# 192 unread TensorE products behind the last product of a two-layer decoder trunk

## The chip, the cores and the metric

The kernel runs on one core of a Trainium2 chip. The metric is the device time of one execution in microseconds (us), lower is better. Five engines work side by side on their own instruction streams: TensorE (PE in the profile; its weight loads are listed apart as PEld), VectorE (DVE), ScalarE (ACT), GpSimd (POOL) and SyncE (SP), which issues most of the DMA transfers.

## The reference

The reference is a decoder trunk of two layers on 256 positions of width 2048, all in float32. The first layer is a Mamba-2 mixer, the second a sliding-window attention with sinks; each ends in a LayerNorm of `ALPHA * x + mixer(x)`. The change concerns nothing that is computed; what stands next to it is the end of the second layer:

```python
def _layernorm(x, g, b):
    mu = jnp.mean(xf, axis=-1, keepdims=True)
    var = jnp.mean(jnp.square(xf - mu), axis=-1, keepdims=True)
    y = (xf - mu) * lax.rsqrt(var + EPS) * g.astype(jnp.float32) + b.astype(jnp.float32)
...
    o = _swa_sink_attention(q, k, v, sinks.reshape(KV_HEADS, Q_PER_KV))
    o = o * jax.nn.silu(gate)
    return o @ w_out
...
        x = _layernorm(ALPHA * x + h, ln_g[layer], ln_b[layer])
```

## The kernel before

**Split products.** Weights come from DRAM in units of 128 x 2048 float32. Each unit is split into two float32r tiles: `wh`, the rounded value (ScalarE, line 178), and `wl`, the rest (VectorE, line 181). Activations are split in the same way (`xH`/`xL`, `x1H`/`x1L`, `yH`/`yL`, `oH`/`oL`). A product of two float32 matrices is then three float32r products, high by high, high by low and low by high, added up in a PSUM tile. Every product loads its own stationary operand.

**Two forms.** In the projections (`narrow` and `mac`, line 265) the weights are stationary, 128 columns of them, and 256 columns of activations move. In the output products (`out_unit`, line 339) the activations are stationary and 512 columns of weights move; the last output tile is done in two halves of 256 columns.

**Places.** The tiles `wh` and `wl` are 2112 elements (8448 bytes) wide: 2048 of a unit and 64 to spare. In most units the data begin at byte 0 of the tile (`WHOLE`). In the attention projections they begin at 64 bytes modulo 256 for all but the first blocks (`BROKEN`, `BROKEN2`). The activation tiles `xH` and `xL` are laid by `Split` so that all but the first block begin at 192 modulo 256; the other activation tiles named above begin at 0.

**The order.** The tile framework schedules what is not pinned by `keep_in_program_order` (`ordered` in the last part); the last part is pinned throughout. `out_last` (line 353) goes over four output tiles `nb` for the first 128 positions and then for the second, with `behind` after each: it takes LayerNorm statistics and, behind the last tile of a half, the norm and the stores. For the second half that is `last` (line 1436): three `ax` PSUM tiles get `b` of the norm by a product with the identity (line 1444), then `t` times the diagonal matrix `dg` (line 1453), while VectorE does the other column blocks (lines 1416 and 1423). The results are stored by SyncE and ScalarE (line 1411). The pool `ax` has four buffers. After the program's own instructions SyncE waits for every DMA queue's count and for the count of each other engine, and a barrier of all engines closes the program (line 1580).

Of the kernel before, what the change touches and what calls it, by code (L numbers as in the profile page):

```python
# [9 lines left out]
F32R = mybir.dt.float32r  # L10
BF16 = mybir.dt.bfloat16
# [6 lines left out]
P = 128  # L18
# [79 lines left out]
def trunk(ctx: ExitStack, tc: tile.TileContext, A: dict, out: bass.AP, dbg=None):  # L98
    nc = tc.nc
# [20 lines left out]
    def mm_tile():  # L120
        return mm_ps.tile([P, 512], F32, tag="mm", name=nm("mm"), bufs=4)
# [136 lines left out]
    def next_unit(behind=False):  # L258
        load_next(min(used[0] + 1 + AHEAD, len(srcs)) - len(units), behind, not behind)
        used[0] += 1  # L260
        return units[used[0] - 1]
# [60 lines left out]
    def pinned(m, pin):  # L322
        if pin:
            tc.keep_in_program_order(m)

    def out_unit(aH, aL, h, u, nb, first, rms=None, pin=False, c0=0, c1=512, add=None, low_last=False):

        ps = mm_tile()[:, : c1 - c0]
        hs = slice(h * P, (h + 1) * P)
        if add is not None:  # L330

            for i in range(2):
                pinned(nc.tensor.matmul(ps, add[0], add[1 + i], start=i == 0, stop=False), pin)
        steps = [(k, a, l) for k in range(4) for a, l in ((aH, 0), (aL, 0), (aH, 1))]
        if low_last:
            steps.sort(key=lambda s: s[1] is aL)
        for n, (k, a, l) in enumerate(steps):
            ks = slice(k * 512 + c0, k * 512 + c1)
            pinned(nc.tensor.matmul(  # L339
                ps, a[:, k, hs], (u.h, u.l)[l][:, ks], start=n == 0 and add is None, stop=n == 11  # L340
            ), pin)
        v = xr[:, h, nb * 512 + c0 : nb * 512 + c1]
        if add is not None:
            return ps
        if first:
            nc.vector.scalar_tensor_tensor(v, v, ALPHA, ps, ALU.mult, ALU.add)
        elif rms is not None:
            nc.vector.scalar_tensor_tensor(v, ps, rms[:, h : h + 1], v, ALU.mult, ALU.add)
        else:
            pinned(nc.vector.tensor_tensor(v, v, ps, ALU.add), pin)  # L350

    def out_last(aH, aL, behind, add):


        us = []
        for nb in range(4):
            us.append(next_unit())
            out_unit(aH, aL, 0, us[nb], nb, False, low_last=nb == 0)
            behind(0, nb)
        for nb in range(4):  # L360

            n = 256 if nb == 3 else 512
            for c0 in range(0, 512, n):
                ps = out_unit(aH, aL, 1, us[nb], nb, False, None, True, c0, c0 + n, add if nb == 3 and c0 else None)
                behind(1, nb, c0, c0 + n, ps)
# [638 lines left out]
    us = {}  # L1004
# [80 lines left out]
    for h in range(2):  # L1085
        ps = mm_tile()
# [317 lines left out]
    ordered = tc.keep_in_program_order  # L1404
# [57 lines left out]
    def behind(h, nb, c0=0, c1=512, v=None):  # L1462
        ordered(norm_stats(st2, h, nb, c0, c1, v))
        if (h, nb) == (0, 3):
            sc[0] = norm_scale(bp, st2, 0, 4)
            centre(0, 0)
            nmr = bp.tile([P, 1], F32, tag="nmr", name="nmr")
            ordered(nc.vector.tensor_scalar(nmr[:], sc[0][0][:, 0:1], sc[0][1][:], -1.0, ALU.mult, ALU.mult))
            scale(0, 0)
            for c in range(1, 4):  # L1470
                norm_aside(0, c, nmr)
        elif (h, nb) == (1, 1):
            norm_aside(0, 3, None)
        elif (h, c0 + c1) == (1, 768):
            last(v)
# [7 lines left out]
    nc.scalar.activation(rH, v, AF.Copy)  # L1483
    nc.vector.tensor_tensor(rL, v, rH.bitcast(F32), ALU.subtract)
    out_last(*os_[3], behind, (one, rH, rL))


def _layout(inputs):
    import numpy as np
# [94 lines left out]
```

## Time and profile before

| | us |
|---|---|
| time, median of 2 runs (975.04 to 975.18) | 975.11 |
| span of the profiled execution, first to last instruction | 973.8 |
| outside the span (median less span) | 1.3 |
| TensorE busy | 965.5 |
| VectorE busy | 786.6 |
| ScalarE busy | 671.4 |

The page of the profile names the span of its execution; the two timed runs are executions of the same program, and the time that each takes in all is that of the table's first row. The time of a matrix product in the profile runs from its start to its modelled end; since products are pipelined, neighbours overlap, and the step from start to start is what one costs. A row of the chain of waits names its start, how long it lasted, the engine, what was written, the line and how many instructions; a timeline row names start, length, engine, line, operation, output and inputs. The granted TensorE clock was 1.000 in the mean of the span.

### The profile page before, as it was taken

How to read it: one execution, taken by the hardware profiler on the slowest of the kernel's cores; microseconds unless marked ns; L12 is line 12 of the kernel's file. 1: busy time of each engine (PE TensorE's matmuls, PEld its weight loads, DVE VectorE, ACT ScalarE, POOL GpSimd, SP SyncE). 2: the span in 40 equal slices, each digit the busy share in tenths (PEclk: the TensorE clock that was granted, in tenths of full speed). 3: DMA queues.
4: the chain of work that ended last, by engine and by line, in shares of the span. 5: the costliest groups of instructions: out<-in, count | busy, mean ns of one | idle time of the engine just before them, and what ended most of it. 6: DMA issues, size and time to landing. Idle time of an engine off the chain costs nothing.

```text
span 973.8 us, 18857 instructions
## 1 busy us (share of the span) xinstructions
PE 965.5 (99%) x7332; PEld 892.0 (92%) x7332; DVE 786.6 (81%) x1217; ACT 671.4 (69%) x1282; POOL 119.1 (12%) x202
## 2 busy tenths in 40 slices
PE   9999999999999999999999999999999999999998
PEld 8999989998999999999899899888999988898976
DVE  7978898896977877787797687889977769778778
ACT  7675884884785686487477579467777776884772
POOL 0000403102110310310300121411000000000002
PEclk9999999999999999999999999999999999999999
DMA  9689467676656666576476654568654545456542
GB/s 359 237 290 337 147 216 228 212 230 203 218 192 220 205 205 206 167 237 213 152 250 203 216 178 155 187 190 265 193 174 158 185 138 186 153 177 213 205 143 86
DMA packets 61273, 197.90 MB, mean 203 GB/s; under 512 B 6800, under 2 KB 11328, under 8 KB 60928
## 3 DMA queue, kind: packets, MB, share of 16 engines
q1 hardware_dynamic: 58528, 188.53, 59.1%
q0 software_dynamic: 2048, 7.65, 2.4%
q8 instruction: 57, 0.93, 0.4%
q10 hardware_dynamic: 608, 0.52, 0.2%
q14 instruction: 32, 0.26, 0.1%
HBM read 194.45 MB, written 2.23 MB: 202 GB/s over the span
## 4 chain that ended last, share of the span: by engine, by line
PE 75%; DVE 10%; ACT 6%; DMA 5%; issue 3%; SPq 1%; DVEq 0%; ACTq 0%
PE mm L265 48%; PE mm L339 20%; DVE wl L181 4%; DMA wr<-in_wa 2%; PE mm L1052 2%; PE ax L670 2%; ACT wh L178 2%; DMA wr<-in_wb 1%; ACT p L1248 1%; DMA xr<-in_first 1%; DVE cv L510 1%; ACT e L566 1%; ACT ptw L1281 1%; ACT pt L1281 0%; DMA rscr<-f 0%
## 5 line engine op out<-in xcount | busy, mean ns | idle before, releaser
L181 DVE TENSOR_TENSOR wl<-wr,wh 128x1024 fp32r<-128x1024 f32 (+2 forms) x354 | 391.5, 1126 | 87.8 <-ACT wh L178 86.0
L178 ACT ACTIVATE wh<-wr 128x1024 fp32r<-128x1024 f32 (+2 forms) x354 | 332.9, 974 | 95.9 <-PE mm L265 50.9
L265 PE MATMUL mm<-xH,wh 128*128 128x256 f32 x1280 | 354.6, 277 | 0.1
L265 PE MATMUL mm<-xH,wl 128*128 128x256 f32 x1280 | 353.8, 276 | 0.0
L265 PE MATMUL mm<-xL,wh 128*128 128x256 f32 x1280 | 353.7, 276 | 0.0
L265 PEld LDWEIGHTS mm<-xH,wh 128*128 128x128 f32 x1280 | 240.3, 188 | 2.3 <-issue 1.0
L265 PEld LDWEIGHTS mm<-xL,wh 128*128 128x128 f32 x1280 | 240.4, 188 | 1.0
L265 PEld LDWEIGHTS mm<-xH,wl 128*128 128x128 f32 x1280 | 240.3, 188 | 0.1
L265 PE MATMUL mm<-x1H,wh 128*128 128x256 f32 x512 | 142.2, 278 | 2.1 <-DVE sg L1186 2.1
L265 PE MATMUL mm<-x1L,wh 128*128 128x256 f32 x512 | 141.6, 277 | 0.0
L265 PE MATMUL mm<-x1H,wl 128*128 128x256 f32 x512 | 141.5, 276 | 0.0
L339 PE MATMUL mm<-wh,yH 128*128 128x512 f32 x256 | 100.8, 394 | 0.1
L339 PE MATMUL mm<-wh,yL 128*128 128x512 f32 x256 | 99.8, 390 | 0.0
L339 PE MATMUL mm<-wl,yH 128*128 128x512 f32 x256 | 99.7, 390 | 0.0
L265 PEld LDWEIGHTS mm<-x1H,wh 128*128 128x128 f32 x512 | 96.1, 188 | 3.6 <-DVE sg L1186 2.4
L265 PEld LDWEIGHTS mm<-x1L,wh 128*128 128x128 f32 x512 | 96.2, 188 | 0.1
L265 PEld LDWEIGHTS mm<-x1H,wl 128*128 128x128 f32 x512 | 96.2, 188 | 0.0
L510 DVE SCALAR_TENSOR_TENSOR cv<-mm,pc,cv 128x255 f32<-128x255 f32 x144 | 68.4, 476 | 4.6 <-ACT cv L508 2.5
L686 POOL TENSOR_TENSOR yz<-yz,z 128x256 f32<-128x256 f32 x32 | 26.7, 843 | 259.2 <-DVE yz L681 259.2
L339 PEld LDWEIGHTS mm<-wl,yH 128*128 128x128 f32 x256 | 48.1, 188 | 10.3
L339 PEld LDWEIGHTS mm<-wh,yH 128*128 128x128 f32 x256 | 48.1, 188 | 9.7 <-issue 0.3
L339 PEld LDWEIGHTS mm<-wh,yL 128*128 128x128 f32 x256 | 48.1, 188 | 9.0
(247 smaller groups left out, 1262.8 us busy)
## 6 DMA issues: line engine op xcount, KB each, us to landing
wr<-in_wa SPq DMA_DIRECT2D x154, 512.0 KB, 5.2
wr<-in_wo SPq DMA_DIRECT2D x64, 512.0 KB, 4.4
wr<-in_wq SPq DMA_DIRECT2D x32, 512.0 KB, 4.4
wr<-in_wg SPq DMA_DIRECT2D x31, 512.0 KB, 4.8
wr<-in_wb SPq DMA_DIRECT2D x16, 512.0 KB, 4.0
wr<-in_wb SPq DMA_DIRECT2D x32, 256.0 KB, 4.3
rb<-rscr SPq DMA_DIRECT2D x11, 512.0 KB, 5.4
wr<-in_wkv SPq DMA_DIRECT2D x8, 512.0 KB, 5.7
```

The costliest lines, as they stand in the source:

```text
L178: m = nc.scalar.activation(h[:, sl], v, AF.Copy)
L181: m = nc.vector.tensor_tensor(l[:, sl], v, h[:, sl].bitcast(F32), ALU.subtract)
L265: m = nc.tensor.matmul(ps, a, b, start=first and i == 0, stop=last and i == 2)
L339: pinned(nc.tensor.matmul(ps, a[:, k, hs], (u.h, u.l)[l][:, ks], start=n == 0 and add is None, stop=n == 11), pin)
L510: nc.vector.scalar_tensor_tensor(a[:, sft:], ps[:, : S - sft], w(3 - sft), a[:, sft:], ALU.mult, ALU.add)
L566: m = nc.scalar.activation(e[:, h, cols], rb[:, h, c * P :], AF.Relu, scale=-1.0, bias=rtk[:, c, h0 + h : h0 + h + 1])
L670: nc.tensor.matmul(ps[64 * r : 64 * r + 64, cols], st.xd[:, c, i, 64 * r : 64 * r + 64], e[:, 256:] if c else e[:, :256], start=c == 0, st ...
L686: nc.gpsimd.tensor_tensor(v, v, st.z[i][:], ALU.mult)
L1052: m = nc.tensor.matmul(ps[:], (x1H, x1L, x1H)[i][:, kk, hs], (u.h, u.h, u.l)[i][:, ks], start=(kk, i) == (0, 0), stop=ui == 3 and (k, i) = ...
L1248: nc.scalar.activation(byhead[:, r], byhead[:, r], AF.Exp, bias=ng[:, r : r + 1], accum_out=rs[:, r : r + 1])
L1281: nc.scalar.copy(to[32 * c : 32 * c + 32].rearrange("p r a -> p (r a)"), src[32 * i : 32 * i + 32, cc_].rearrange("p r b -> p (r b)"),)
```

## The change

Behind the last part of the kernel 192 products are written. They read the split weights of the third unit of `out_last`, `wh` as moving and `wl` as stationary operand, each from its 64th element on (256 bytes), and all write one more `ax` tile, each as a complete product (`start` and `stop` set). Nobody reads it. `at` is the offset of the moving operand in bytes, `w_at` that of the stationary one. Eleven values of `at` and six other pairs are taken with 512 columns, six products each, eight of the same values of `at` with 256 columns, eight products each. Then come six products with 64 and six with 32 stationary columns, and six and eight with both operands read as bfloat16, 512 and 256 columns. `last_units` only makes the units of `out_last` known outside it.

```diff
+    last_units = []
+
     def out_last(aH, aL, behind, add):
-        us = []
+        us = last_units
         for nb in range(4):
             us.append(next_unit())
...
     out_last(*os_[3], behind, (one, rH, rL))
+
+    mv, st = last_units[2].h, last_units[2].l
+    ps = ax_tile()
+
+    def unread(times, n, at, w_at, m=P, dt=F32R):
+        per = 4 if dt is F32R else 2
+        for _ in range(times):
+            a, b = mv[:, 64:1088].bitcast(dt), st[:, 64:320].bitcast(dt)
+            ordered(nc.tensor.matmul(
+                ps[:m, :n], b[:, w_at // per : w_at // per + m], a[:, at // per : at // per + n], start=True, stop=True
+            ))
+
+    for at in (0, 16, 32, 48, 64, 96, 128, 160, 192, 224, 240):
+        unread(6, 512, at, 0)
+    for at, w_at in ((0, 32), (0, 64), (0, 128), (0, 192), (64, 64), (64, 128)):
+        unread(6, 512, at, w_at)
+    for at in (0, 32, 64, 96, 128, 160, 192, 224):
+        unread(8, 256, at, 0)
+    unread(6, 512, 0, 0, 64)
+    unread(6, 512, 0, 0, 32)
+    unread(6, 512, 0, 0, P, BF16)
+    unread(8, 256, 0, 0, P, BF16)
```

The end of TensorE's stream before; `t` and `gb` are the tiles of the last norm, `cc` holds the identity:

```order
L339 MATMUL mm_11412<-wl_11273,oH_11166 128x256
L1444 MATMUL ax_11428<-gb_1_11236,cc 128x256
L1444 MATMUL ax_11429<-gb_1_11236,cc 128x256
L1444 MATMUL ax_11430<-gb_1_11236,cc 128x512
L1453 MATMUL ax_11428<-t_11442,dg 128x256
L1453 MATMUL ax_11429<-t_11442,dg 128x256
L1453 MATMUL ax_11430<-t_11450,dg 128x512
L1580 UNCONDITIONAL_BRANCH
```

The last product of a norm block is followed by the branch to the closing barrier. The same place in the changed kernel, where these lines stand two further down and `x102` counts equal rows in a run; the bfloat16 products at the end have weight loads of their own, of which the first pair is shown:

```order
L339 MATMUL mm_11412<-wl_11273,oH_11166 128x256
L1446 MATMUL ax_11428<-gb_1_11236,cc 128x256
L1446 MATMUL ax_11429<-gb_1_11236,cc 128x256
L1446 MATMUL ax_11430<-gb_1_11236,cc 128x512
L1455 MATMUL ax_11428<-t_11442,dg 128x256
L1455 MATMUL ax_11429<-t_11442,dg 128x256
L1455 MATMUL ax_11430<-t_11450,dg 128x512
L1496 MATMUL ax_11465<-wh_11245,wl_11246 128x512 x102
L1496 MATMUL ax_11465<-wh_11245,wl_11246 128x256 x64
L1496 MATMUL ax_11465<-wh_11245,wl_11246 64x512 x6
L1496 MATMUL ax_11465<-wh_11245,wl_11246 32x512 x6
L1496 LDWEIGHTS wl_11246
L1496 MATMUL ax_11465<-wh_11245,wl_11246 128x512
```

The new products stand behind the last product of the norm, line 1453 before and 1455 now, and ahead of the branch to the closing barrier. Nothing else changes place on any engine.

## The prediction

> **What bounds the kernel now.** I read the page first, then the chain of waits, then the last ten microseconds in the timeline, because the change stands there.
>
> ```profile
> span 973.8 us, 18857 instructions
> PE 965.5 (99%) x7332; PEld 892.0 (92%) x7332; DVE 786.6 (81%) x1217; ACT 671.4 (69%) x1282; POOL 119.1 (12%) x202
> PE 75%; DVE 10%; ACT 6%; DMA 5%; issue 3%; SPq 1%; DVEq 0%; ACTq 0%
> L265 PE MATMUL mm<-xH,wh 128*128 128x256 f32 x1280 | 354.6, 277 | 0.1
> L339 PE MATMUL mm<-wh,yH 128*128 128x512 f32 x256 | 100.8, 394 | 0.1
> ```
>
> TensorE bounds nearly all of it: 99% busy, 75% of the chain, and its big groups wait for nothing (0.1 us). What a product costs is not the 277 or 394 ns of its own time, since the next one begins before it ends. It is the distance from start to start, which the chain of waits gives for long unbroken stretches:
>
> ```profile
> 321.86 27.23 PE mm L265 x240
> 349.09 5.45 PE mm L339 x24
> 354.54 10.91 PE mm L265 x96
> ...
> 835.64 32.99 PE mm L265 x288
> ```
>
> 27.23 / 240 = 0.1135 us for a product of 256 columns, 5.45 / 24 = 0.227 us for one of 512. These are split float32 (float32r) products, and each loads its own stationary operand; the loads are hidden. Now the end:
>
> ```profile
> 964.07 0.28 PE L339 MATMUL mm<-wh,oL 128*128 128x256 f32 x1
> ...
> 965.27 0.28 PE L339 MATMUL mm<-wl,oH 128*128 128x256 f32 x1
> 965.39 1.88 PE L1444 MATMUL ax<-gb,cc 128*128 128x256 f32 x6
> 967.39 1.99 PE L1453 MATMUL ax<-t,dg 128*128 128x256 f32 x6
> 969.42 0.58 ACT L1454 COPY xr<-ax 128x512 f32<-128x512 f32 x1 [0.49 <-PE ax L1453]
> 970.01 0.88 DVE L1423 SCALAR_TENSOR_TENSOR xr<-t,rs,gb 128x256 f32<-128x256 f32 x2
> L1411 SPq DMA_DIRECT2D out<-xr x8: 332/333/400, 958.9 to 970.9; - x8
> DMA to landing us min/median/max: 1.9/2.0/2.1
> SPq L1580 <- DMA out<-xr: 1.1, 3, 0.4
> ```
>
> TensorE ends at 967.39 + 1.99 = 969.38. VectorE ends at 970.89, the last store is issued at 970.9 and lands 2.0 later, at 972.9; SyncE waits for it (last row), and the closing barrier of all engines takes the 0.9 to 973.8. So TensorE stands idle for the last 4.4 us, and that is all the cover that work put behind its last product can have. The median of the two runs is 975.11, so 1.3 us lie outside the span of the profiled execution; I carry them over unchanged.
>
> **The change part by part.** Nothing is removed or moved. One engine, TensorE, gets 192 products behind the L1453 ones. The moving operand is `wh`, the stationary one `wl`, of the third unit of the last output block; both were written and used before 963, so nothing is waited for. The target is an `ax` buffer that the end of the kernel does not hold. Nobody reads the results; but SyncE's closing waits include TensorE's count, which now comes with the last of the 192. No instruction of another engine changes place, so the stores are as before and are over by 972.9.
>
> *How many.* With 512 columns: 11 x 6 at eleven places of the moving operand, 6 x 6 at other places of the stationary one, 6 each with 64 and 32 stationary columns, 6 bfloat16: 66 + 36 + 12 + 6 = 120. With 256 columns: 8 x 8 and 8 bfloat16: 72.
>
> *Where they start.* A product begins about 0.16 before its predecessor's time ends (0.28 long and 0.12 apart in the 964 rows). So the first begins near 969.38 - 0.16 = 969.22. TensorE is the engine that finishes earliest here; from 969.22 on every product moves its end, and from about the 16th (972.9) the end of the kernel.
>
> *What one costs.* The rows show that the place matters. Both `wh` and `wl` are 8448 bytes wide, 33 x 256, and start at multiples of 256 bytes in the built program, so offsets can be told modulo 256. The first stretches with 256 columns have the moving `xH`, `xL` at 192 and the stationary weights at 0: 0.1135. The stretch from 835.64 has the moving `x1H`, `x1L` at 0 and nearly all weights at 64: 32.99 / 288 = 0.1145. The 964 rows have both operands at 0: (965.27 - 964.07) / 10 = 0.120. The 512-column rows of L339 have both at 0 as well: 0.227. The floor is what streaming alone takes. The six L1444 passes are full float32, at half rate: 4 of 256 and 2 of 512 columns, 2048 columns in 1.88 - 0.16 = 1.72 us, 0.84 ns a column, so 0.42 at full rate, 0.215 for 512 and 0.1075 for 256. A float32r product thus pays 0.006 over the floor at a good pair of places and 0.012 with both at 0. I take that excess to be the same for 512 columns (0.012 is seen: 0.227 - 0.215) and, for the untried pairs, the middle: 0.224 for 512 and 0.117 for 256. Ends: the floors, and 0.227 and 0.120; a pair could be worse than any seen, which the upper end of the range must hold.
>
> The Trainium skill ("TensorE: Matmul & The Clock Gate", Step-by-step) says that the weight load reads SBUF by a port of its own and does not steal from the running matmul, so that places should not matter; by its warm gap of N/2.4 + 2.5 ns (Back-to-back issue gap) the 192 would take an estimated 120 x 0.2158 + 72 x 0.1092 = 33.8 us. The 0.1135 against 0.120 of the rows speaks against it: same engine, same width, other places.
>
> *Fewer stationary columns.* Streaming is by moving columns, and the load of 64 columns is shorter than that of 128:
>
> ```profile
> L670 PEld LDWEIGHTS ax<-e,xd 128*64 128x64 f32 x256 | 16.0, 137 | 5.6
> L265 PEld LDWEIGHTS mm<-xH,wh 128*128 128x128 f32 x1280 | 240.3, 188 | 2.3 <-issue 1.0 <-ACT wh L212 0.4
> 232.47 0.28 PE L265 MATMUL mm<-xL,wh 128*128 128x256 f32 x1
> 232.59 0.28 PE L265 MATMUL mm<-xH,wl 128*128 128x256 f32 x1
> 232.79 0.76 PE L670 MATMUL ax<-e,xd 128*64 128x256 f32 x6
> ```
>
> So 0.215 to 0.227 each; I take 0.222. A change between 128 and 64 columns costs once (0.20 at 232.59 where 0.11 is usual): three such changes, 128 to 64 to 32 to 128, 0.27 us.
>
> *bfloat16.* Before has it only in the fill at the start, six in this row:
>
> ```profile
> 1.39 2.55 PE L388 MATMUL ax<-zero 128*128 128x512 bf16 x6
> 4.63 0.39 PE L265 MATMUL mm<-xH,wh 128*128 128x256 f32 x1
> 4.89 0.38 PE L265 MATMUL mm<-xL,wh 128*128 128x256 f32 x1
> 5.11 0.36 PE L265 MATMUL mm<-xH,wl 128*128 128x256 f32 x1
> ```
>
> Five of 512 columns in about 2.55 - 0.42 = 2.13, 0.426 each, in a stretch where 256 float32r columns too take 0.22 to 0.26, twice their later price. Half of it is 0.213; between that and 0.227 I take 0.217, and 0.110 for 256. Their explicit weight loads stand between the products as the implicit ones do, and hide alike.
>
> *Sum.* 102 x 0.224 = 22.85; 12 x 0.222 = 2.66; 64 x 0.117 = 7.49; 6 x 0.217 = 1.30; 8 x 0.110 = 0.88; changes 0.27: 35.45 us. The last product's own time outlasts its step by 0.16. TensorE ends at 969.22 + 35.45 + 0.16 = 1004.8. Behind that SyncE's last waits and the barrier: 0.9 as before, and about 0.1 to see the count: span 1005.8. With 1.3 outside it: **1007.1 us**, 32 more, 3.3% slower. At the floors everywhere (25.8 + 7.74 = 33.5, no changes) it is 1005.2; at the dearest prices seen everywhere (120 x 0.227 + 72 x 0.120 + 0.27 = 36.2) 1007.9.
>
> **The rivals.** About 2% (19.5 us, up to 994.6) is what a measurement of this kernel tells from no change.
>
> *Overlap in pairs: not slower.* If products whose results do not depend on each other ran two at a time, they would end on the other side of 994.6. That this happens on TensorE at all is in the row of L1328:
>
> ```profile
> 933.95 1.08 PE L1328 MATMUL ax<-pt,vt 128*64 128x512 f32 x4
> ```
>
> Four half-rate passes of 512 columns would take 4 x 0.43 = 1.7 in a row and take 1.08: two halves of the array, 64 columns each, run at once. Were the added ones paired likewise: 60 x 0.227 + 36 x 0.12 = 17.9, TensorE ends at 987.3, the time is 989.6, 1.5% over. It decides if the average step falls below about 0.12 us. Against it: all but 12 of the 192 use 128 columns, the 12 the same columns each time, and all write the same bank. 2%. The Trainium skill (same page, Back-to-back issue gap) states a sustained 131 ns for 512 columns in streams of load and matmul, by which the 192 take an estimated 120 x 0.131 + 72 x 0.1 = 23 us and the time is 994.7, just at the bound; the 0.227 of L339 in exactly such a stream disagrees.
>
> *Dropped or never waited for.* If unread products were left out, the time stays 975. The fill of L388 writes an `ax` that nobody reads, and it is in the trace; 1%.
>
> *Loads that show.* If the weights of the same tile could not be loaded under the running product, each would pay something like the 0.09 of a change of columns: 192 x 0.09 = 17 more, 1024. Loads hide in each of the 240 products of a stretch; but there the operands alternate, here the same address comes again. 3%.
>
> *A pair of places far worse than any seen.* Should half of the places (some 90 products) pay 0.05 more, the time is 1011.5. The rows know only three pairs (0 and 0, 192 and 0, 0 and 64). 8%.
>
> *The clock falls.* TensorE idles less than 0.15 us before the first added product, and the granted clock stays whole even after the engine stops:
>
> ```profile
> 969.00:971.00 2.00, 0.38 (x1) 0.00 (x0) 1.85 (x4) 0.58 (x1) 0.00 (x0) 1.00 0.76 281
> 971.00:973.00 2.00, 0.00 (x0) 0.00 (x0) 0.00 (x0) 0.00 (x0) 0.00 (x0) 1.00 0.67 244
> ```
>
> At half clock the 35 us become 70 and the time 1042; 1%.
>
> **How the numbers follow.** The forecast has 85%. 1005 to 1011 holds it and part of the worse pairs, together over 8 in 10. Slower by over 2%: 85 + 8 + 3 + 1 = 97%. Within 2%: pairs and dropped, 3%. Faster has no mechanism, under 0.5%.
>
> **What would show it.** In the profile after: 7332 + 192 = 7524 TensorE products, the new ones on one line from 969.2 to about 1004.8 without idle time; a chain that ends on that line; stores that land at 972.9 as before; steps of 0.22 and 0.115. It is wrong if the steps differ by more than 0.012 among the places, if the loads show as gaps, or if the span ends more than 1.2 us behind the last product.

## The result, and the profile after

The changed kernel took 1007.79 us (median of 2 runs, 1007.72 to 1007.85) against 975.11: ratio 1.0334, 95% interval 1.0314 to 1.0353. It is slower by 32.7 us. Forecast were 1007.1 and 32.

The page of the changed kernel, then the end of its chain of waits (start, length, what, how many), then what SyncE waited for at the very end:

```profile
span 1006.1 us, 19241 instructions
PE 1001.8 (100%) x7523; PEld 924.2 (92%) x7524; DVE 787.3 (78%) x1217; ACT 671.4 (67%) x1282; POOL 120.0 (12%) x202
PE 94%; DVE 3%; ACT 2%; issue 1%; DVEq 0%; ACTq 0%
966.95 1.99 PE ax L1455 x6
968.93 33.99 PE ax L1496 x178
1002.93 0.07 issue
1003.00 2.12 PE ax L1496 x13
SPq L1604 <- PE ax L1496: 33.3, 1, 33.3
```

The chain now ends on the new line, 1496, and it is one piece: 178 float32r products and behind them the bfloat16 ones (one of 192 records is missing in the trace), ending at 1005.12. The stores come out as before: the last copy of VectorE ends at 970.45, and then SyncE waits 33.3 us for TensorE alone:

```profile
969.57 0.88 DVE L1425 SCALAR_TENSOR_TENSOR xr<-t,rs,gb 128x256 f32<-128x256 f32 x2
973.00:1004.00 31.00, 30.93 (x166) 25.18 (x166) 0.00 (x0) 0.00 (x0) 0.00 (x0) 1.00 0.00 1
```

The second row is a stretch of the windows view (PE, PEld, DVE, ACT, POOL busy, clock, DMA): 31 us in which only TensorE works, at the whole clock. The steps, from two rows of the timeline, one among the eleven places for 512 columns, one among the 256 columns and one of 64 stationary columns:

```profile
979.69 2.03 PE L1496 MATMUL ax<-wh,wl 128*128 128x512 f32 x8
992.82 6.86 PE L1496 MATMUL ax<-wh,wl 128*128 128x256 f32 x57
1000.92 1.55 PE L1496 MATMUL ax<-wh,wl 128*64 128x512 f32 x6
```

A row of n products lasts n - 1 steps and one product's own time (0.39 for 512 columns, 0.28 for 256). So the steps are (2.03 - 0.39) / 7 = 0.234, (6.86 - 0.28) / 56 = 0.1175 and (1.55 - 0.39) / 5 = 0.232. Over all 102 products of 512 columns the starts lie 0.2324 apart, from 0.224 to 0.241; the bfloat16 ones 0.2158 and 0.1093, within 1 ns.

So the sum of the steps is close and one of its terms is not understood: 512 float32r columns cost 0.232 here and 0.227 in L339. The experiments ask for the cover first and then for that. One of the ten runs of the first experiment took 1628.75 us at a mean granted clock of 0.556, and the ratio given there leaves it out.

### The profile page after: what moved, and what is told of

The parts are those of the page before. It is cut to its first block, busy times and chain, and to the rows that moved or that the text cites. A ratio compares the mean times of both kernels' runs of the same rounds, so it can differ in the third digit from the quotient of the medians.

```text
span 1006.1 us, 19241 instructions
## 1 busy us (share of the span) xinstructions
PE 1001.8 (100%) x7523; PEld 924.2 (92%) x7524; DVE 787.3 (78%) x1217; ACT 671.4 (67%) x1282; POOL 120.0 (12%) x202
## 4 chain that ended last, share of the span: by engine, by line
PE 94%; DVE 3%; ACT 2%; issue 1%; DVEq 0%; ACTq 0%
PE mm L265 59%; PE mm L339 24%; PE ax L1496 4%; PE ax L672 2%; PE mm L1054 2%; DVE wl L181 1%; ACT p L1250 1%; PE ax L609 0%; ACT wh L178 0%; PE ax L1222 0%; PE mm L408 0%; ACT ptw L1283 0%; PE ax L985 0%; PE ax L1215 0%; PE ax L390 0%
## 5 line engine op out<-in xcount | busy, mean ns | idle before, releaser
L265 PE MATMUL mm<-xH,wh 128*128 128x256 f32 x1280 | 355.2, 277 | 0.0
L265 PE MATMUL mm<-xL,wh 128*128 128x256 f32 x1280 | 354.2, 277 | 0.0
L265 PE MATMUL mm<-xH,wl 128*128 128x256 f32 x1280 | 354.1, 277 | 0.0
L265 PEld LDWEIGHTS mm<-xH,wh 128*128 128x128 f32 x1280 | 240.7, 188 | 1.8 <-ACT wh L212 0.3
L265 PEld LDWEIGHTS mm<-xL,wh 128*128 128x128 f32 x1280 | 240.7, 188 | 1.0
L265 PEld LDWEIGHTS mm<-xH,wl 128*128 128x128 f32 x1280 | 240.6, 188 | 0.0
L265 PE MATMUL mm<-x1H,wh 128*128 128x256 f32 x512 | 143.0, 279 | 2.0 <-DVE sg L1188 2.0
L265 PE MATMUL mm<-x1L,wh 128*128 128x256 f32 x512 | 142.4, 278 | 0.0
L265 PE MATMUL mm<-x1H,wl 128*128 128x256 f32 x512 | 142.3, 278 | 0.0
L339 PE MATMUL mm<-wh,yH 128*128 128x512 f32 x256 | 100.7, 393 | 0.0
L265 PEld LDWEIGHTS mm<-x1H,wh 128*128 128x128 f32 x512 | 96.9, 189 | 3.6 <-DVE sg L1188 2.4
L339 PE MATMUL mm<-wl,yH 128*128 128x512 f32 x256 | 99.8, 390 | 0.0
L339 PE MATMUL mm<-wh,yL 128*128 128x512 f32 x256 | 99.8, 390 | 0.0
L265 PEld LDWEIGHTS mm<-x1L,wh 128*128 128x128 f32 x512 | 96.9, 189 | 0.1
L265 PEld LDWEIGHTS mm<-x1H,wl 128*128 128x128 f32 x512 | 97.0, 189 | 0.0
L339 PEld LDWEIGHTS mm<-wl,yH 128*128 128x128 f32 x256 | 48.0, 188 | 10.2
L339 PEld LDWEIGHTS mm<-wh,yH 128*128 128x128 f32 x256 | 48.1, 188 | 9.4 <-DVE xr L348 0.2
L339 PEld LDWEIGHTS mm<-wh,yL 128*128 128x128 f32 x256 | 48.1, 188 | 9.0
```

Of the source, the lines that this page charges most:

```text
L265: m = nc.tensor.matmul(ps, a, b, start=first and i == 0, stop=last and i == 2)
L339: pinned(nc.tensor.matmul(ps, a[:, k, hs], (u.h, u.l)[l][:, ks], start=n == 0 and add is None, stop=n == 11), pin)
```

## The experiments

Each replaces the calls of `unread` and leaves the kernel ahead of them as it is. In the diffs `tm` is `nc.tensor.matmul`, `mv_` and `st_` are slices of `wh` and `wl` of the third unit at the given bytes behind the 256th, `h2` and `l2` are their first 512 and 128 columns there, and `ps` is the unread `ax` tile. "Settled" is the mean of the last twelve steps of a group of 24.

### Twelve products: is there cover?

```diff
-    for at in (0, 16, 32, 48, 64, 96, 128, 160, 192, 224, 240):
-        unread(6, 512, at, 0)
...
+    unread(12, 512, 0, 0)
```

> 12 of the 192 products are kept: 512 columns, both operands at byte 0. Theory of the cover: TensorE is idle from about 969 on, the stores land at 972.9; 12 steps of 0.232 us take 2.8, TensorE ends near 972 and the time stays 975.1, ratio 1.000. Rival (every product lengthens the kernel by its step, there is no cover): 975.1 + 2.8 = 977.9, ratio 1.003.

Measured: 975.04 us against 975.27 of the kernel before, ratio 1.000, interval 0.9991 to 1.001. The chain's last rows, and the last store's source on VectorE:

```profile
966.34 1.99 PE ax L1455 x6
968.33 2.77 PE ax L1496 x12
...
968.96 0.88 DVE L1425 SCALAR_TENSOR_TENSOR xr<-t,rs,gb 128x256 f32<-128x256 f32 x2
```

TensorE ends at 971.10 and VectorE at 969.84; the span is 973.2 though, since the last store is issued at 969.9 and the median time to landing was 2.4 us. The chain as inferred names TensorE only because its work ended last; 2.8 us of products cost nothing. The cover is as forecast, and the rival's 977.9 lies outside the interval.

### All of them bfloat16: is the excess one of float32r?

```diff
-        unread(6, 512, at, 0)
+        unread(6, 512, at, 0, P, BF16)
```

(and so for every call)

> All 192 products read their operands as bfloat16, with the same offsets in bytes, counts and columns. Theory: the excess over streaming is one of float32r alone: 120 x 0.216 + 72 x 0.109 = 33.8 us in place of 36.2, time 1007.8 - 2.4 = 1005.4. Rival (the excess is one of these places, whatever the type): 1007.8, and steps of 0.225 to 0.235 and 0.117 in the trace.

Measured: 1005.66 us, ratio 1.0313 (1.0296 to 1.0331). The interval overlaps the changed kernel's, so the trace decides. Its chain:

```profile
969.57 0.22 PE ax L1496
...
991.42 9.96 PE ax L1496 x76
1001.39 0.16 issue
1001.54 2.12 PE ax L1496 x13
```

From 969.57 to 1003.66 are 34.1 us where the changed kernel takes 36.2 (968.93 to 1005.12). Every step at all seventeen pairs of places is 0.215 or 0.216 for 512 columns and 0.109 or 0.110 for 256 (four of the 192 records are missing). So the excess comes with float32r, and the places play no part for bfloat16. What it is in float32r is not told apart by this: the bfloat16 operands have half the bytes, and their weight loads are instructions of their own. The saving is 2.1 and not 2.4, since bfloat16 pays for each change of the number of stationary columns (0.16 of issue before the last row, and steps of 0.20 and 0.31 at the other two), which float32r does not.

### Nine kinds of operands: why 0.232 here and 0.227 in L339?

```diff
+    for i in range(24):
+        ordered(tm(ps, l2, h2, start=True, stop=True))
+    for i in range(24):
+        ordered(tm(ps, l2, h2, start=i == 0, stop=i == 23))
+    for i in range(24):
+        ordered(tm(ps, u2.l[:, i % 4 * 128 : i % 4 * 128 + 128], h2, start=True, stop=True))
...
```

> Nine groups of 24 float32r products of 512 columns in place of the 192, one source line each, to find why the steps were 0.232 where L339 has 0.227 at the same places. In order: (1) as in the changed kernel; (2) the same, accumulated; (3) four stationary blocks of wl in turn; (4) three blocks of wh moving in turn; (5) stationary oH; (6) stationary wh of the fourth unit; (7) L339's own pattern, oH/oL against wh/wl, accumulated by twelve; (8) the same, each with start; (9) one block of oH against one of wh. Quiet end (the steps are longer since the other engines stand still): all nine 0.232. Operands (which tiles, or that the same ones come again): (7) and (8) 0.227, and the group that first falls to 0.227 among (2) to (6) and (9) names the cause: (2) accumulation, (3) or (4) repetition, (5), (6), (9) the stationary tile.

Measured, the chain, which has one row for each group: the first two and the last three; the four between them have 5.44 as well:

```profile
969.28 5.47 PE ax L1506 x24
974.75 5.44 PE ax L1508 x24
...
1001.95 5.44 PE ax L1519 x24
1007.39 5.44 PE ax L1522 x24
1012.83 5.44 PE ax L1524 x24
```

5.44 / 24 = 0.2267 in eight of nine, 0.228 in the first. Both theories fall: the quiet end, the operands, accumulation and repetition leave the settled step as it is. What differs is inside the first group. The distances from start to start are, from its second product on and in ns:

```
230 231 236 228 233 231 226 227 227 226 227 227 226 227 227 226 227 227 226 227 227 226
```

After six uneven steps it settles at 226, 227, 227, over and over. All later groups have both operands at 0 modulo 256 and never leave that rhythm. The changed kernel changes the place every six products. A third theory came from this: a step has to settle after each change of places.

### Fourteen groups: columns, places of 256, and 32 stationary columns

```diff
+    for _ in range(24):
+        ordered(tm(ps[:, :320], st_(0), mv_(0, 320), start=True, stop=True))
...
+    for _ in range(24):
+        ordered(tm(ps[:, :256], st_(0), mv_(192, 256), start=True, stop=True))
...
```

> Fourteen groups of 24 float32r products, wh moving and wl stationary. First 256, 320, 384, 448 and 512 columns, both at 0: if the excess over streaming (0.4167 ns a column and 2.5 ns a product from the bfloat16 steps 0.109 and 0.216) is paid for each moving column, it grows evenly from 8 to 16 ns; if it is paid for each weight load, it is the same in all five. Then 256 columns with moving and stationary at (192, 0), (0, 64), (64, 128), (128, 192), (0, 0), (64, 0), (128, 0): if the difference of the places modulo 256 decides, the first four are alike at 0.113 and the last three lie at 0.117 to 0.120; if the place itself decides, the four differ. Last 32 stationary columns with 256 moving, at (0, 0) and (192, 0): if the weight load collides, the first is nearer the floor of 0.109 than the 128 columns are; if not, 0.117 and 0.113 again.

Measured, the chain: 256, 320, 384, 448 and 512 columns; then 256 at (192,0), and at (0,0); then 32 stationary columns at (0,0) and (192,0):

```profile
969.54 2.87 PE ax L1511 x24
972.40 3.52 PE ax L1513 x24
975.92 4.16 PE ax L1515 x24
980.09 4.95 PE ax L1517 x24
985.04 5.49 PE ax L1519 x24
990.53 2.83 PE ax L1521 x24
...
1001.84 2.87 PE ax L1529 x24
...
1010.39 2.73 PE ax L1535 x24
1013.12 2.74 PE ax L1537 x24
```

Settled steps: 0.120, 0.1467, 0.1733, 0.2067, 0.2267. Less the streaming of the expectation that is 11, 11, 11, 17 and 11 ns: it is paid once for a product and not for each column, with 448 out of line. The four pairs with a difference of 192 are alike, but at 0.1178 and not at 0.113; (64,0) has 0.1178 too, (128,0) 0.119. With 32 stationary columns it is 2.73 / 24 = 0.114 at both places, settled 0.1133: at (0,0) fewer stationary columns take away 7 of the 11 ns. That the load of the weights is what costs them is argued and not shown.

That (192,0) settles at 0.1178 contradicts the changed kernel, whose (192,0) group ended in steps of 113 and 114 ns. The next three runs go after both findings.

### One place for all

```diff
-    for at in (0, 16, 32, 48, 64, 96, 128, 160, 192, 224, 240):
+    for at in (0,) * 11:
...
-    for at, w_at in ((0, 32), (0, 64), (0, 128), (0, 192), (64, 64), (64, 128)):
+    for at, w_at in ((0, 0),) * 6:
...
-    for at in (0, 32, 64, 96, 128, 160, 192, 224):
+    for at in (192,) * 8:
```

> As the changed kernel, but all 102 products of 512 columns have both operands at 0 and all 64 of 256 columns have the moving operand at 192; counts, columns and types stay. Settling (a step settles some ten products after the offsets last changed, as in the first group of the run with nine groups: 0.230 to 0.236, then 0.2267): the 102 take 102 x 0.2267 + 0.05 = 23.2 us in place of 23.7, and the 64 settle at 0.113 to 0.118; time 1007.8 - 0.5 = 1007.3, ratio 1.0328. Place alone (each pair of offsets has its own step, changes cost nothing): 102 x 0.2305 = 23.5 us, and no run of equal steps.

Measured: 1006.98 us, ratio 1.0325 (1.0308 to 1.0342), by itself not to be told from the changed kernel. The chain's long row and the timeline at the place shown above:

```profile
968.72 33.48 PE ax L1496 x178
979.70 1.98 PE L1496 MATMUL ax<-wh,wl 128*128 128x512 f32 x8
```

33.48 against 33.99, 0.51 us less where 0.5 was expected, and (1.98 - 0.39) / 7 = 0.227. The 102 products settle within the first ten; the 64 stay at 0.1178. So the changes of place cost 0.5 us. But this does not tell whether settling or the other pairs' own steps take it.

### Eleven pairs for 512 columns

```diff
+    for _ in range(24):
+        ordered(tm(ps[:128, :512], st_(0, 128), mv_(192, 512), start=True, stop=True))
...
```

> Eleven pairs of places for 512 float32r columns and 128 stationary ones, 24 products each: (moving, stationary) at (0,0), (192,0), (64,0), (128,0), (32,0), (16,0), (0,64), (64,64), (0,128), (96,0), (224,0) bytes; then 64 and 32 stationary columns at (0,0) and 32 at (192,0). Settling: each group starts with some ten uneven steps of 0.224 to 0.240 and then repeats one value; (0,0) and (64,64) 0.2267. If the offset modulo 256 matters for 512 columns too, some pair settles at 0.220 (8 fewer cycles at 1.2 GHz) or above 0.2267; if not, all settle at 0.2267. With 32 stationary columns 0.220, as 256 columns went from 0.120 to 0.113; if the load plays no part, 0.2267.

Measured: the chain for (0,0), (192,0), (64,0), (128,0), (32,0), further on for (64,64), and for 64 and 32 stationary columns at (0,0):

```profile
969.45 5.47 PE ax L1511 x24
974.92 5.60 PE ax L1513 x24
980.52 5.50 PE ax L1515 x24
986.02 5.57 PE ax L1517 x24
991.60 5.60 PE ax L1519 x24
...
1008.36 5.46 PE ax L1525 x24
...
1030.57 5.52 PE ax L1533 x24
1036.10 5.56 PE ax L1535 x24
```

Settled: (0,0) and (64,64) 0.2267 and 0.2268, (64,0) 0.229, (16,0) 0.232, (128,0) and (0,128) 0.233, (192,0), (32,0), (0,64), (96,0) and (224,0) 0.233. No pair is under 0.2267. Not every group starts unevenly or comes to rest: (192,0) has 0.232 to 0.234 from its first step on, and (128,0) still goes through steps of 0.228 to 0.241 at its end, so that its value is a mean. Place makes up most of what the changed kernel has above 0.2267: for the twelve of its seventeen pairs that have a group of 24 here or in the last run below, the settled steps average 0.2316 and its own 0.2322. Settling shows where the place is good: its (0,0) group, six products long, had 0.2305. Fewer stationary columns do not help 512 moving ones at (0,0): 0.230 and 0.232. That part of the expectation fails, and with it the load as the only cause.

### What runs ahead

```diff
+    for _ in range(2):
+        for _ in range(8):
+            ordered(tm(ps[:128, :256], st_(0, 128), mv_(160, 256), start=True, stop=True))
+        for _ in range(24):
+            ordered(tm(ps[:128, :256], st_(0, 128), mv_(192, 256), start=True, stop=True))
...
```

> 256 float32r columns with the moving operand at 192 and the stationary one at 0, 24 products at a time, three times over with different work ahead: 8 products of 256 columns at (160,0); 24 of 512 at (0,0); 24 of 256 at (0,0); and the whole row twice. Entry decides (one pair of places has more than one settled step, and what ran before picks it): 0.113 behind the (160,0) products, as in the changed kernel, 0.118 behind the 512 columns, as in the run of fourteen groups. Place decides: the same settled step all six times.

Measured, the first of two equal rounds: (160,0), (192,0), 512 columns, (192,0), (0,0), (192,0):

```profile
968.69 0.94 PE ax L1512 x8
969.64 2.74 PE ax L1514 x24
972.38 5.46 PE ax L1516 x24
977.83 2.83 PE ax L1518 x24
980.66 2.87 PE ax L1520 x24
983.53 2.74 PE ax L1522 x24
```

The same products at the same places take 2.74, 2.83 and 2.74: settled 0.1133 behind 256 columns and 0.1178 behind 512. The second round repeats it to 0.01 us. Entry decides for this pair. It also weakens a reading of the run of fourteen groups: the four pairs with one difference follow one another there, so that they may be alike because the rhythm was handed on. For 512 columns the difference has the next run to stand on.

### Finer places, and where the results go

```diff
+    for _ in range(24):
+        ordered(tm(ps[:128, :512], st_(16, 128), mv_(16, 512), start=True, stop=True))
...
+    for i in range(24):
+        ordered(tm((ps, ps2)[i % 2], st_(0), mv_(192, 512), start=True, stop=True))
```

> 512 float32r columns, 24 products at each of (moving, stationary) = (0,0), (4,0), (8,0), (0,4), (0,8), (0,16), (0,32), (0,240), (16,16), (192,192), (192,128) bytes; then (0,0) and (192,0) with the results going to two PSUM tiles in turn; then 256 columns at (0,0) going to the two halves of one tile in turn. If it is the difference of the places that decides, (0,0), (16,16) and (192,192) settle at 0.2267, and (192,128) like (64,0) at 0.229; if the place itself does, (16,16) and (192,192) differ from (0,0). A pair at 0.220 would be a better one for L339 than its present (0,0). If the PSUM writes are behind the excess, two tiles in turn lower the steps from 0.2267 and 0.2333, and two halves from 0.120; if the reads are, nothing changes.

Measured, the chain for (4,0), (16,16), (192,192), (192,128), and then (192,0) with two PSUM tiles in turn and 256 columns with two halves in turn:

```profile
973.62 5.67 PE ax L1514 x24
...
1012.68 5.54 PE ax L1528 x24
1018.23 5.45 PE ax L1530 x24
1023.68 5.49 PE ax L1532 x24
...
1034.65 5.60 PE ax L1536 x24
1040.25 2.87 PE ax L1538 x24
```

(4,0) is the worst, 0.2367 settled; the pairs not shown, (0,0) aside, lie from 0.228 to 0.233. (192,192) is as (0,0), and (192,128) as (64,0), but (16,16) is 0.231: for 512 columns the difference decides among the multiples of 64 bytes tried, not below. Where the results go plays no part: 5.60 and 2.87 as with one tile. L339 stands at the best step found, so no faster version came out of this.

## Why the prediction was right

*What bounds the end.* Right. TensorE idles while the stores go out, and the twelve products showed that the first 2.8 us are free. Behind that the steps count, and SyncE's wait for TensorE replaces its wait for the stores.

*Where they start.* The rule (0.16 before the end of the last L1455 product) holds: that ends at 966.95 + 1.99 = 968.94, and the second new product starts at 969.00, one step after 968.78 (the record of the first begins earlier, at 968.37, and overlaps the last L1455 pass). The forecast 969.22 is missed by 0.44 only because this execution was ahead by so much when it reached the place.

*What one costs.* The term that was mis-sized is the 0.224 for 512 columns; it measured 0.2324, and so for the narrow ones 0.232 in place of 0.222: 102 x 0.0084 + 12 x 0.010 = 1.0 us more. The step that failed is "I take that excess to be the same for 512 columns ... and, for the untried pairs, the middle". From 256 columns, where (0,0) is the dearest place, it was concluded that (0,0) is dear for 512 too and others are cheaper. It is the other way round: for 512 columns (0,0) is, with (64,64) and (192,192), the cheapest of all pairs tried, and the others lie at 0.228 to 0.237. The upper end of 0.227 was thereby too low; the time stayed inside the range all the same, since the sum at the dearest prices (1007.9) charged 0.227 and 0.120 to the bfloat16 products and to the cheaper places of 256 columns too, and the range went on to 1011 for worse pairs. Why the places matter stays open. The 0.117 for 256 columns measured 0.1175 and the bfloat16 prices of 0.217 and 0.110 measured 0.2158 and 0.109.

One reading behind this was wrong: the 0.1145 for moving at 0 and stationary at 64. TensorE waits ahead of the row at 835.64, so the row holds the first product's own time, and (32.99 - 0.28) / 287 = 0.1140; the second product also comes 0.222 behind the first, and from the sixth step on the trace has 0.113, 0.113 and 0.114 over and over, as in the first stretches, but for one or two steps of 0.119 to 0.121 in every 48. So the rows of before knew two prices for 256 columns and not three, and (192,0) and (0,64), which have the same difference modulo 256, had the same one.

*Changes of the number of columns.* 0.27 us were put in and float32r paid next to nothing: the step into the 64 columns is 0.120 and the one out of them 0.230. The 0.20 read from the row at 232.59 came with a change from float32r to full float32 as well. This took back a quarter of the miss above.

*The end.* The span ends 0.96 behind the last product (1.0 forecast), 1006.1 against 1005.8.

*The sum.* That the span is only 0.3 above the forecast is partly luck: 1.0 too little for the steps stands against 0.27 too much for changes and a start that came 0.44 earlier. The other 0.4 of the 0.7 lies outside the span, where 1.3 was carried over as the median of two runs less the span of one execution. In the profiled run of the changed kernel it is 1007.85 - 1006.1 = 1.75, and in all runs on record that have both numbers 1.7 to 2.5, the kernel before included.

*The types.* With 512 columns float32r takes 11 to 21 ns more than bfloat16 from start to start (0.2267 to 0.2367 against 0.2158), by places. The warm gap of N/2.4 + 2.5 ns that the Trainium skill states ("TensorE: Matmul & The Clock Gate", Back-to-back issue gap) holds to a nanosecond for the bfloat16 products, and not for float32r. The Trainium skill also says ("TensorE: Matmul & The Clock Gate", Step-by-step) that the weight load does not steal from the running matmul; the part that the places play for float32r speaks against it, but that load and product collide was not shown, since at (0,0) 32 stationary columns helped 256 moving ones and not 512. The 131 ns for 512 columns that the Trainium skill states as well ("TensorE: Matmul & The Clock Gate", Back-to-back issue gap) appeared nowhere: no added product of 512 columns had a step under 0.215.

*The rivals.* None came true. The worse pairs did come, with 0.010 at most above the dearest row and not the 0.05 of that rival. The clock did fall, but far ahead of the added products (last section), and not under them.

## What to carry to other kernels

Work behind the last product of a kernel is free only as long as stores are still landing, here 3.7 us by the rows (969.22 to 972.9), of which 2.8 were tried; read that from the last landing and the closing barrier, not from the busy share. A product's price is the step from start to start in a long stretch, and for float32r it depends on the places of both operands, on the number of columns and on what ran before: a price read at 256 columns does not carry over to 512. A probe needs two dozen equal products, since up to ten pass before the steps settle, and some pairs of places go through a cycle instead of one step.

## What the runs showed of the hardware that was not expected

One pair of places has two settled steps, 0.1133 and 0.1178 for 256 columns, and the products ahead pick one, repeatably. Why is open. The long L265 stretches of the kernel run at 0.1133 already. Many settled steps are whole multiples of 6.67 ns: the five at (0,0) for 256 to 512 columns, 0.120, 0.1467, 0.1733, 0.2067 and 0.2267, are 18, 22, 26, 31 and 34 of them (448 columns lie one above the line of the other four), and 0.1133 and 0.2333 are 17 and 35. Others are means of a cycle and lie between, such as 0.1178 and the 0.229 of (64,0).

The granted clock fell by half in the middle of the changed kernel and not in the profile of before. The windows view of the changed kernel, then of before at the same work:

```profile
835.20:838.50 3.30, 3.30 (x18) 3.30 (x17) 1.91 (x2) 3.21 (x9) 0.00 (x0) 0.50 0.69 243
835.60:838.90 3.30, 3.26 (x28) 3.26 (x29) 2.32 (x3) 3.21 (x9) 0.00 (x0) 1.00 0.67 227
```

It follows the 2.0 us for which TensorE waits in both kernels for L1186 (L1188 in the changed one), far ahead of the change. Of the eight experiments' profiles four have it as well, at the same work, four have not. The block of 288 products in which it falls takes 34.61 us instead of 32.99, 1.6 more; but later waits of TensorE shrink. From the start of that block (834.82 in the changed kernel, 835.64 before) to the first L1455 or L1453 product (966.95 and 967.39) it is 132.1 us against 131.75: 0.4 are left. All five profiles with the fall have 132.1 to 132.3 for this stretch, all five without it 131.7 to 131.8. The timed runs hint at more: with all products bfloat16 the runs with a mean clock of 0.998 took 1006.15 and 1006.40 us, those with 1.000 took 1005.13 and 1005.17. Both runs of the changed kernel had 0.998, the profile of before 1.000, so up to about 1 us of the 32.7 may belong to the clock and not to the products; no run here separates the two.
